# A decoder layer in split fp32: the residual held over the norm's factor, the last down blocks by seven products, one group summed in PSUM through ScalarE, and order constants by stage

## The chip, the cores and the metric

The kernel runs on one core of one Trainium2 chip. The metric is the device time of one execution in microseconds, with the median over several runs. TensorE (PE) multiplies, VectorE (DVE), ScalarE (ACT) and GpSimd (POOL) work on the tiles in between, and SyncE (SP) issues most of the DMA transfers. One execution was profiled; its span is shorter than its time by what lies before the first and behind the last instruction.

## The reference, cut to what matters

One step of a decoder layer for 512 prompt tokens and 8 x 4 sample tokens, 544 columns in all, with a model width of 1024 and a feed-forward width of 2816, in fp32:

```python
h = rmsnorm(x, norm_mix)
z = h @ w_in                                   # split into dilated attention and HGRN2
...
x = x + jnp.concatenate([att, o], axis=-1) @ w_out
c = rmsnorm(x, norm_cross)
...
x = x + co @ w_co                              # cross attention
u = rmsnorm(x, norm_ffn)
ug = u @ w_gate
up = jnp.concatenate([conv_buf.astype(ug.dtype), ug], axis=1)
conv = conv_b + sum(conv_w[j] * up[:, j:j + T] for j in range(CONV_W))
x = x + (jax.nn.silu(conv) * (u @ w_up)) @ w_down
...
yp = rmsnorm(yp, norm_final)
```

## The kernel before, in words

All activations lie transposed: a tile has 128 features as partitions and the 544 tokens as columns. x is held as eight tiles `xr` (m = 0 to 7), and the feed-forward's inner width of 2816 is 22 blocks of 128 (k = 0 to 21), whose activations are called `up`, and, once they are split for PE, `h0h`, `h0l` to `h21h`, `h21l`.

**Split products.** An fp32 product is made of three passes in PE's format fp32r: high by high, high by low and low by high (`passes`). So each operand is split: ACT casts the high part (a name that ends in h), DVE subtracts it for the low part (a name that ends in l). Some small products (norm sums, attention scores, the recurrence) are plain fp32 matmuls.

**Seven products.** Where two blocks of output rows and two halves of the columns (of `HT` = 272) meet, a two by two product of blocks is made by seven products in place of eight (the Winograd form of Strassen's method). `Pair` does this for gate and up, two output blocks at a time: the weight's sums S1 and S3 are made by DMA (a load by SP and an accumulating load on POOL's queue), S2 and S4 by DVE; the differences W, X, T, U, V of the right side are made once (`blocks`). The products are q1 to q7, with 12 matmuls each, in PSUM tiles called ps_a, ps_d, ps_c. For the first gate pair the weights are `wrg` (A11, A12; high `whg`, low `wlg`), `S1g`, `S2g`, `S3g` and their parts `S1g2h`, `S3g2h`, `S3g2l`; the products go to `ps_ag`.

**The feed-forward.** `ffn_in` gives the rows' factor r (tile `r_ux`, 1 over the root mean square, made by ACT as Exp of -0.5 times a Ln). Blocks 0 and 1 of gate and up are plain products, the others are pairs. `conv` takes a gate block (tile `ug`), applies the convolution's taps on ACT and DVE (tile `cv`), silu on ACT, and then multiplies by r once more (`weigh`), so that up's product needs no factor of its own; POOL fills the edges of `ug` and keeps its last columns (`last`). The down product is summed into x in groups of four k blocks (`DOWNS`; the last is k = 14 to 17), in two column cuts `CUTS` of 256 and 288, each with a DVE add of PSUM into `xr` (`down_half`), PSUM tile `ps_d`. These halves are laid between the products of the pairs by a fixed table.

**The end.** The last four blocks, k = 18 to 21 (`DOWN_LAST`), follow by `last_half(m, c)`: 12 matmuls for each m and column half, first all m of half 0 (288 columns), then half 1 (256), PSUM tile `ps_dz`. Each result is added to x on DVE, squared on ACT and summed over m (tile `acc_final`) by POOL, for the last m by DVE. `final(c)` adds the partitions up by two plain fp32 matmuls (`psr_final`), ACT makes the factor (`r_fin` and `r_final`: Ln, then Exp twice, once into PSUM), DVE and POOL make the outputs y, and SP and ACT issue the stores. `final(0)` comes after m = 2 of half 1. The very last half is added by PE onto a copy of x that ACT put into PSUM.

**What sets the order.** A recorder, `Tape`, takes every instruction as a step with its needs, and sets the order of each engine. PE's steps that are marked as main keep their written order; its other steps (mostly plain fp32) are put between them in bursts. `BURST` says how much such work must be ready for a burst and `PATIENCE` how long it may wait. `due` gives each step a time before which it has to begin: `MARGIN` is the room that it keeps ahead of a main step, and `LEAD` says how long ahead of its due time an engine may take a step, unless the step has a lead of its own (`lead=`, `tape.early`). All engines work off their queues in order, so a step that waits holds back all that stands behind it on its engine, DMA issues on SP and POOL included.

Almost all instructions go through one recording line (L638) and all DMA issues through another (L612), so the profile's groups are told apart by their tiles. In the changed kernel these are L650 and L624.

## Time and profile before

| what | value |
|---|---|
| median of 3 runs | 818.39 us (816.56 to 819.32) |
| profiled execution | 817.74 us |
| its span | 816.0 us, so 1.74 us lie outside |
| PE busy | 803.5 us, 98% |
| PE weight loads (PEld) | 755.0 us, 93% |
| DVE busy | 656.3 us, 80% |
| ACT busy | 424.7 us, 52% |
| POOL busy | 108.3 us, 13% |
| feed-forward with the last blocks | about 460 to 807.65 us |
| last blocks (ps_dz) | 782.57 to 807.65 us |

The page gives busy time and share of the span. Rows of a timeline give start, length, engine, line, operation, out<-in with shapes and count, and in brackets how long the engine idled before it and what ended that. Matmuls overlap: a row's own length, 0.28 us, is more than the step from one matmul to the next, which is what counts for time and is read from starts. In rows of windows a stretch is followed by busy us and count of PE, PEld, DVE, ACT and POOL, then PE's granted clock, the DMA engines' share and GB/s.

### The profile page before, as it was taken

The numbers are of one execution on the slowest core, as the hardware profiler recorded it, in microseconds if no ns is written. First come the engines' busy times: TensorE is split into PE (matmuls) and PEld (weight loads), VectorE is DVE, ScalarE is ACT, GpSimd is POOL, SyncE is SP. The second block draws the span as 40 slices with busy tenths as digits, with TensorE's granted clock in tenths as the row PEclk, the third lists the DMA queues.
The fourth block names the chain that finished last, engine by engine and source line by source line (L and its number), as shares of the span: only waits on it lengthen the run. The fifth ranks groups of instructions, "written<-read, shape, count | busy, mean of one in ns | idle before, by whom it ended". The sixth has DMA issues, their size and how long they took to land.

```text
span 816.0 us, 18919 instructions
## 1 busy us (share of the span) xinstructions
PE 803.5 (98%) x7515; PEld 755.0 (93%) x7515; DVE 656.3 (80%) x1486; ACT 424.7 (52%) x845; POOL 108.3 (13%) x186
## 2 busy tenths in 40 slices
PE   9999999999999999999999999999999999999996
PEld 9999986797889889999889999999999999999996
DVE  6986789987997987564679999997888788887854
ACT  7643346366558455454457656544454455445543
POOL 0020000010010000002300221222113111211013
PEclk9999999999999999999999999999999999999999
DMA  9439996956844444261732665555455565564403
GB/s 315 165 101 306 335 382 204 318 168 215 259 137 134 146 132 157 59 219 36 236 109 61 167 171 133 155 130 167 118 154 132 132 166 142 130 166 119 136 17 111
DMA packets 93065, 135.48 MB, mean 166 GB/s; under 512 B 6320, under 2 KB 60336, under 8 KB 92976
## 3 DMA queue, kind: packets, MB, share of 16 engines
q1 hardware_dynamic: 86208, 122.79, 46.9%
q0 software_dynamic: 5760, 10.49, 8.3%
q8 instruction: 59, 0.97, 0.5%
q10 hardware_dynamic: 1008, 0.99, 0.4%
q14 instruction: 30, 0.25, 0.1%
...
## 4 chain that ended last, share of the span: by engine, by line
PE 61%; DVE 4%; ACT 1%; DMA 1%; issue 0%; DVEq 0%
PE ps_d L638 13%; PE ps_ag L638 7%; PE ps_au L638 7%; PE ps_wo L638 6%; PE ps_cu L638 4%; PE ps_cg L638 4%; PE ps_co L638 3%; PE ps_dz L638 3%; PE ps_cq L638 3%; PE ps_dg L638 2%; PE ps_du L638 2%; PE ps_g L638 1%; DVE wl L638 1%; PE ps_cpo L638 1%; PE ps_cp L638 1%; PE ps_cv L638 1%
## 5 line engine op out<-in xcount | busy, mean ns | idle before, releaser
L638 ACT CAST wh<-wr 128x1024 fp32r<-128x1024 f32 (+1 forms) x54 | 46.4, 873 | 51.5 <-PE ps_z_i L638 10.8
L638 DVE TENSOR_TENSOR wl<-wr,wh 128x1024 fp32r<-128x1024 f32 (+1 forms) x54 | 55.2, 1030 | 3.0 <-ACT wh L638 2.8
L638 DVE TENSOR_TENSOR xr<-xr,ps_d 128x256 f32<-128x256 f32 x80 | 34.7, 434 | 13.7 <-PE ps_d L638 12.9
L638 POOL COPY last<-ug 128x2 f32<-128x2 f32 (+1 forms) x44 | 19.9, 479 | 129.2 <-DVE ug L638 129.2
L638 DVE SCALAR_TENSOR_TENSOR cv<-ug,vec,cv 128x560 f32<-128x560 f32 x44 | 35.2, 799 | 0.8
L638 ACT ACTIVATE cv<-ug,vec 128x560 f32<-128x560 f32 x22 | 18.8, 856 | 29.9 <-DVE ug L638 29.9
L638 POOL TENSOR_TENSOR hvm<-hsm,cs 64x512 f32<-64x512 f32 x4 | 5.5, 1386 | 160.4 <-ACT hsm L638 116.1
L638 DVE TENSOR_TENSOR cv<-cv,r_ux 128x512 f32<-128x512 f32 (+1 forms) x44 | 18.4, 436 | 3.4 <-ACT cv L638 3.0
L612 POOL DMA_DIRECT2D S1u<-in_w_up x10 | 8.6, 862 | 92.8 <-PE ps_au L638 62.0
L638 POOL TENSOR_SCALAR cp<-cp,cden 128x256 f32<-128x256 f32 x8 | 8.0, 999 | 93.2 <-DVE cden L638 93.0
L638 POOL COPY ug<-conv_state 128x16 f32<-128x16 f32 x22 | 18.4, 837 | 13.9 <-PE ps_co L638 5.8
L638 ACT ACTIVATE cv<-cv 128x560 f32<-128x560 f32 x22 | 14.8, 673 | 8.5 <-DVE cv L638 8.2
L638 DVE TENSOR_TENSOR keptg<-ps_cg,keptg 128x272 f32<-128x272 f32 x20 | 8.8, 440 | 12.7 <-PE ps_cg L638 12.2
L638 PE MATMUL ps_co<-coh,wh 128*128 128x256 f32 (+1 forms) x64 | 18.9, 295 | 0.0
L638 ACT ACTIVATE P<-P,mx 128x128 f32<-128x128 f32 (+3 forms) x32 | 17.6, 552 | 1.8 <-DVE mx L638 1.8
L638 PE MATMUL ps_co<-col,wh 128*128 128x256 f32 (+1 forms) x64 | 18.4, 288 | 0.0
L638 PE MATMUL ps_co<-coh,wl 128*128 128x256 f32 (+1 forms) x64 | 18.4, 288 | 0.0
L638 DVE TENSOR_TENSOR xr<-xr,ps_wo 128x256 f32<-128x256 f32 (+1 forms) x16 | 6.8, 436 | 13.7 <-PE ps_wo L638 13.6
L638 DVE TENSOR_TENSOR keptu<-ps_cu,keptu 128x272 f32<-128x272 f32 x20 | 8.8, 438 | 9.9 <-PE ps_cu L638 9.7
L638 DVE TENSOR_TENSOR xr<-xr,ps_dz 128x288 f32<-128x288 f32 (+1 forms) x15 | 6.6, 438 | 12.4 <-PE ps_dz L638 12.4
L638 PE MATMUL psdo<-st,dpt 128*32 128x256 f32 x224 | 16.3, 387 | 0.0
L638 ACT COPY keptg<-ps_ag 128x272 f32<-128x272 f32 x20 | 7.7, 386 | 16.3 <-PE ps_ag L638 16.2
...
## 6 DMA issues: line engine op xcount, KB each, us to landing
...
wd<-in_w_down SPq DMA_DIRECT2D x32, 256.0 KB, 3.4
...
```

What stands on the lines that cost most here:

```text
L612: return tape.put(engine, lambda: call(*args, **kw), outs, ins, 0.1, 0.3, size)
L638: return tape.put(engine, lambda: call(*args, **kw), outs, ins, length, lag, size, port, words)
```

## The change

1. **The residual over the factor.** `weigh` goes. The inner activations are thereby larger by 1/r for each token, and x is brought to the same scale: each `xr` tile is once multiplied by the root mean square (`rms_ffn`, made by ACT as one more Exp of the same Ln), after the pairs' differences have read it and ahead of its first down add. The final norm doesn't see a factor of a token, except in its epsilon, which is folded into the sum of squares: POOL rescales the sum of the ffn norm (`acc_ux`) by epsilon, adds a constant, and the last norm's sum is built on that tile.
2. **Last blocks.** The pairs m = (0,1), (2,3), (4,5) are made by seven products of 6 matmuls of 272 columns each; m = 6 and 7 stay plain. Their weight sums (tiles `wzS`) are made by 20 SP loads (with the plain ones) in place of 8 and 21 accumulating DMAs of 128 KB on POOL's queue; the right side's differences are `lX`, `lU`, `lT`, `lV`. `LAST_ORDER` gives the order of the products; `final(0)` stands ahead of the last two. All y of half 0 are made by DVE.
3. **Group 14.** For k = 14 to 17 ACT copies x into PSUM, PE adds to it, and ACT copies the sum back to `xr`; DVE adds nothing. All down halves are cut into 272 and 272 columns.
4. **Constants by stage.** `BURST`, `PATIENCE`, `LEAD` and `MARGIN` are taken from a table of ten stages of the planned time.

Instructions per engine: PE 6431 to 6413, DVE 1488 to 1467, ACT 802 to 843, POOL 191 to 211, SP 350 to 362.

```diff
-LAST_CUTS = ((0, 288), (288, 256))
+LAST_CUTS = ((0, HT), (HT, HT))
+LAST_ORDER = ((0, 1), (0, 2), (1, 1), (1, 2), (0, 6), (0, 7), (1, 6), (2, 1), (0, 4), (1, 7), (2, 2), (2, 6), (1, 4), (2, 7),
+              (0, 5), (1, 5), (2, 4), (0, 3), (2, 5), None, (1, 3), (2, 3))
...
-    BURST, PATIENCE, SLACK, LEAD, MARGIN = 0.77, 3.65, 12.0, 16.11, 3.44
+    SLACK = 12.0
+    STAGES = ((0.0, 1.05, 3.03, 18.1, 2.34), (60.0, 0.96, 2.87, 17.03, 5.98), (120.0, 1.23, 4.33, 13.64, 2.85),
...
+              (740.0, 0.66, 3.38, 13.88, 4.81))
...
     class SumSq:
...
-    ssq3 = SumSq("final", nc.gpsimd)
+    ssq3 = SumSq("final", nc.gpsimd, acc=ffn_in.ssq.acc)
+    nc.gpsimd.tensor_scalar(ssq3.acc[:, :N], ssq3.acc[:, :N], EPS, D / 128 * EPS * EPS, op0=ALU.mult, op1=ALU.add)
...
-        def weigh():
-            c = hid[j]
-            nc.vector.tensor_tensor(c[:, :SEQ], c[:, :SEQ], r_ffn[:, :SEQ], op=ALU.mult)
-            nc.vector.tensor_tensor(seg(c)[:, :, 0:4], seg(c)[:, :, 0:4], by_batch(r_ffn[:, SEQ:N]), op=ALU.mult)
...
     def down_half(k0, k1, m, c, split, deps):
-        n0, n = CUTS[c]
...
+        n0, n = HT * c, HT
+        on = k0 >= 14
...
+        def fill():
+            box["ps"] = PF(f"ps_d{k0}_{m}_{n0}")
...
+            nc.scalar.copy(box["ps"][:, :n], x[m][:, n0:n0 + n])
...
+        if m not in scaled:
+            scaled[m] = job(lambda: nc.vector.tensor_tensor(x[m][:, :N], x[m][:, :N], rms_ffn[:, :N], op=ALU.mult),
+                            *(d for told in read for d in told.values()), lead=40.0)
+        if k0 >= 14:
+            job(lambda: nc.scalar.copy(x[m][:, n0:n0 + n], box["ps"][:, :n]), p)
+        else:
+            job(lambda: add_to(m)(box["ps"], n0, n), p, scaled[m])
...
-    ON_POOL = (1, 3, 6), (1, 5)
+    k0, k1 = DOWN_LAST
+    ON_POOL = (), (1, 3)
...
+    def last_weights(p):
...
+        nc.gpsimd.dma_start(raw["S13"][:, 0:2, :], w[1][:, 0:2, :], accum_op=ALU.add)
+        nc.gpsimd.dma_start(raw["S13"][:, 2:4, :], w[1][:, 0:2, :], accum_op=ALU.add)
...
+        for to in (slice(0, 2), slice(2, 4)):
+            nc.sync.dma_start(raw["S24"][:, to, :], w[1][:, 0:2, :])
+        for to in (slice(0, 2), slice(2, 4)):
+            nc.gpsimd.dma_start(raw["S24"][:, to, :], w[1][:, 2:4, :], accum_op=ALU.add)
+            nc.gpsimd.dma_start(raw["S24"][:, to, :], w[0][:, 0:2, :], accum_op=ALU.add)
+        nc.gpsimd.dma_start(raw["S24"][:, 2:4, :], w[0][:, 2:4, :], accum_op=ALU.add)
...
+    PRODUCTS = {1: ("a", "A11", "B11"), 2: ("d", "A12", "B21"), 6: ("a", "S2", "U"), 7: ("c", "S3", "X"),
+                5: ("a", "S1", "T"), 4: ("c", "A22", "V"), 3: ("a", "S4", "B22")}
...
+        def product(self, i):
+            bank, wa, xb = PRODUCTS[i]
...
+            for m, c, op, ends in {1: ((m0, 0, ALU.add, False),), 2: ((m0, 0, ALU.add, True),),
+                                   6: ((m1, 0, ALU.subtract, False),),
+                                   7: ((m1, 1, ALU.add, False),), 4: ((m1, 0, ALU.add, True),),
+                                   5: ((m1, 1, ALU.subtract, True),), 3: ((m0, 1, ALU.add, True),)}[i]:
...
+                nc.vector.tensor_tensor(x[m][:, cut], x[m][:, cut], ps[:, :HT], op=op)
```

Where it moves instructions, at these places. First ACT at the start of the feed-forward, where the first gate pair's weights are cast (`whg` for q1, `S3g2h` for a later product); before:

```order
L638 ACTIVATE cv_1217<-ug_1214,vec 128x560
L638 CAST S1g2h<-S1g_1239 128x512
L638 CAST S3g2h<-S3g_1254 128x512
L638 CAST whg_1231<-wrg_1230 128x1024
L638 ACTIVATE cv_1217<-cv_1217 128x560
L638 CAST S2g2h<-S2g_1240 128x512
```

and now:

```order
L650 ACTIVATE cv_1217<-ug_1214,vec 128x560
L650 CAST S1g2h<-S1g_1239 128x512
L650 CAST whg_1231<-wrg_1230 128x1024
L650 ACTIVATE cv_1217<-cv_1217 128x560
L650 CAST S2g2h<-S2g_1240 128x512
L650 CAST S3g2h<-S3g_1254 128x512
```

The cast of S3g now stands behind those of the pair's other weights. DVE at the same place, now:

```order
L650 TENSOR_TENSOR S2g_1240<-S1g_1239,wrg_1230 128x512
L650 TENSOR_TENSOR up_1220<-ps_u_256_1222,cv_1211 128x256
L650 TENSOR_TENSOR up_1220<-ps_u_256_1222,cv_1211 128x32
L650 TENSOR_TENSOR S1g2l<-S1g_1239,S1g2h 128x512
L650 TENSOR_TENSOR wlg_1232<-wrg_1230,whg_1231 128x1024
L650 TENSOR_TENSOR S2g2l<-S2g_1240,S2g2h 128x512
L650 TENSOR_TENSOR up_1228<-ps_u_0_1229,cv_1217 128x256
L650 TENSOR_TENSOR S3g2l<-S3g_1254,S3g2h 128x512
```

Before, the last add to up_1220, S2g, S3g2l and wlg followed each other. Next, DVE from the last adds to x up to the second half's norm (the first y of half 1); before:

```order
L638 TENSOR_TENSOR xr_915<-xr_915,ps_dz_1_2046 128x256
L638 SCALAR_TENSOR_TENSOR y_0_2050<-xr_913,vec,r_final_2049 128x288
L638 SCALAR_TENSOR_TENSOR y_0_2051<-xr_915,vec,r_final_2049 128x288
L638 TENSOR_TENSOR xr_916<-xr_916,ps_dz_1_2055 128x256
L638 SCALAR_TENSOR_TENSOR y_0_2052<-xr_917,vec,r_final_2049 128x288
L638 SCALAR_TENSOR_TENSOR y_0_2053<-xr_918,vec,r_final_2049 128x288
L638 TENSOR_TENSOR xr_917<-xr_917,ps_dz_1_2057 128x256
L638 SCALAR_TENSOR_TENSOR y_0_2054<-xr_920,vec,r_final_2049 128x288
L638 TENSOR_TENSOR xr_918<-xr_918,ps_dz_1_2059 128x256
L638 TENSOR_TENSOR xr_919<-xr_919,ps_dz_1_2062 128x256
L638 TENSOR_TENSOR acc_final<-acc_final,sq_final_5_2060 128x256
L638 TENSOR_TENSOR acc_final<-acc_final,sq_final_6_2063 128x256
```

and now:

```order
L650 TENSOR_TENSOR xr_915<-xr_915,ps_az_2050 128x272
L650 SCALAR_TENSOR_TENSOR y_0_2081<-xr_913,vec,r_final_2080 128x272
L650 TENSOR_TENSOR xr_917<-xr_917,ps_az_2066 128x272
L650 SCALAR_TENSOR_TENSOR y_0_2082<-xr_914,vec,r_final_2080 128x272
L650 TENSOR_TENSOR acc_ux<-acc_ux,sq_final_5_2089 128x272
L650 SCALAR_TENSOR_TENSOR y_0_2083<-xr_915,vec,r_final_2080 128x272
L650 TENSOR_TENSOR xr_919<-xr_919,ps_z_1_2091 128x272
L650 TENSOR_TENSOR acc_ux<-acc_ux,sq_final_6_2090 128x272
L650 SCALAR_TENSOR_TENSOR y_0_2084<-xr_916,vec,r_final_2080 128x272
L650 SCALAR_TENSOR_TENSOR y_0_2085<-xr_917,vec,r_final_2080 128x272
L650 TENSOR_TENSOR acc_ux<-acc_ux,sq_final_7_2092 128x272
```

Five products y, three adds and three sums now alternate ahead of the second norm's sum; three more y follow. The last place is ACT's queue ahead of the last blocks (`ps_d_7` are the PSUM tiles of group 14's last m), now:

```order
L650 COPY ps_d_7_0_1997<-xr_920 128x272
L650 COPY xr_919<-ps_d_6_272_1988 128x272
L650 CAST wzS24h_2031<-wzS_2025 128x512
L650 CAST lXh<-lX 128x544
L650 COPY ps_d_7_272_1998<-xr_920 128x272
L650 CAST lUh<-lU 128x544
L650 CAST wzAh_2058<-wzA_2054 128x512
L650 CAST h21h<-up_1977 128x544
```

The cast of the summed weights S24 of the first pair stands there ahead of the fill of the last PSUM tile and of h21h.

More of the change, by code (lines that the diff above doesn't have):

```diff
@@ L384, in as_written, with at @@
         return self.mark("kept")
+    def at(self, t):
+        return [c for c in self.STAGES if c[0] <= t][-1][1:]
     def due(self):
@@ L550, in order @@
                     at = clock[0] + min(now - clock[1], 4.0)
-                    can = [s for s in waiting[e] if s.ready <= now + 1e-9 and s.begin <= at + (s.lead or self.LEAD) and fits(s)]
+                    ahead = self.at(clock[0])[2]
+                    can = [s for s in waiting[e] if s.ready <= now + 1e-9 and s.begin <= at + (s.lead or ahead) and fits(s)]
                     if can:
@@ L561, in order @@
                     first = now
-                if side and (burst or not main or sum(s.length for s in side) >= self.BURST
-                             or now - first > self.PATIENCE
+                enough, patience = self.at(clock[0])[:2]
+                if side and (burst or not main or sum(s.length for s in side) >= enough
+                             or now - first > patience
                              or min(s.begin for s in side) < clock[0] + now - clock[1]):
@@ L2303, in tile_decoder_step @@
     later.run()
-    r_fin, last_sq = A("r_fin"), A("sq_last")
-    hs, k = [hid[j] for j in range(*DOWN_LAST)], DOWN_LAST[1] - DOWN_LAST[0]
-    ys, last = {}, []
-    ON_POOL = (1, 3, 6), (1, 5)
+    r_fin, last_sq, ys = A("r_fin"), A("sq_last"), {}
+    k0, k1 = DOWN_LAST
+    ON_POOL = (), (1, 3)
     def y_at(m, c):
@@ new lines, in done, with plain_weights @@
+    def done(m, c):
+        cut = slice(HT * c, HT * c + HT)
+        if (m, c) == (5, 0):
+            nc.scalar.activation(last_sq[:, cut], x[m][:, cut], AF.Square)
+        else:
+            ssq3.add(x[m][:, cut], HT * c, nc.vector if (m, c) in ((3, 0), (2, 1), (4, 1), (6, 1)) else None)
+        if m in ON_POOL[c]:
+            nc.scalar.activation(y_at(m, c), x[m][:, cut], AF.Copy, scale=V("norm_final", m))
+    def plain_weights(m):
+        t, hi, lo = (A(f"{n}z{m}", [128, k1 - k0, 128], dt) for n, dt in (("wd", F32), ("wdh", F32R), ("wdl", F32R)))
+        nc.sync.dma_start(t, w_down[m][:, 128 * k0:128 * k1].rearrange("p (k c) -> p k c", c=128))
+        nc.scalar.copy(hi, t)
+        nc.vector.tensor_tensor(lo, t, hi.bitcast(F32), op=ALU.subtract)
+        return [(hi[:, i, :], lo[:, i, :]) for i in range(k1 - k0)]
@@ L2326, in last_half, with plain @@
+    def plain(m, c):
+        cut = slice(HT * c, HT * c + HT)
+        ps = PF(f"ps_z{m}_{c}")[:, :HT]
+        whole = (m, c) == (KT - 1, 1)
         if whole:
             tape.gate_at = len(tape.mains) - 1
-            nc.scalar.copy(ps[:, :n], x[m][:, cut])
+            nc.scalar.copy(ps, x[m][:, cut])
             tape.gate_at = None
+        tape.cut()
         with tape.main():
-            passes(ps, held[m], hs, n0, n, range(k), not whole, loose=whole)
+            passes(ps, held[m], [hid[j] for j in range(k0, k1)], HT * c, HT, range(k1 - k0), not whole, loose=whole)
+        tape.cut()
@@ L2344, in final @@
+        done(m, c)
     def final(c):
-        n0, n = LAST_CUTS[c]
-        cut = slice(n0, n0 + n)
+        cut = slice(HT * c, HT * c + HT)
         ps = PX(f"psr_final{c}")
         for i, sq in enumerate((ssq3.acc, last_sq)):
-            nc.tensor.matmul(ps[:, :n], C("ones"), sq[:, cut], start=i == 0, stop=i == 1)
-        nc.scalar.activation(r_fin[:, cut], ps[:, :n], AF.Ln, bias=eps, scale=1.0 / D)
-        r = PX(f"r_final{c}")[:, :n]
+            nc.tensor.matmul(ps[:, :HT], C("ones"), sq[:, cut], start=i == 0, stop=i == 1)
@@ L2353, in final @@
+        nc.scalar.activation(r_fin[:, cut], ps[:, :HT], AF.Ln, scale=1.0 / D)
+        r = PX(f"r_final{c}")[:, :HT]
         nc.scalar.activation(r, r_fin[:, cut], AF.Exp, scale=-0.5)
@@ L2362, in final @@
             (nc.scalar if c and m % 2 else nc.sync).dma_start(yT[128 * m:128 * m + 128, cut], out)
-    held = []
-    for m in range(KT):
-        t, hi, lo = (A(f"{n}z{m}", [128, k, 128], dt) for n, dt in (("wd", F32), ("wdh", F32R), ("wdl", F32R)))
-        with tape.early(12.0):
-            nc.sync.dma_start(t, w_down[m][:, 128 * DOWN_LAST[0]:128 * DOWN_LAST[1]]
-                              .rearrange("p (k c) -> p k c", c=128))
-            nc.scalar.copy(hi, t)
-            nc.vector.tensor_tensor(lo, t, hi.bitcast(F32), op=ALU.subtract)
-        held.append([(hi[:, i, :], lo[:, i, :]) for i in range(k)])
-        last_half(m, 0)
-    for m in range(KT):
-        last_half(m, 1)
-        if m == 2:
+    pairs_z = [LastPair(p) for p in range(3)]
+    last, held = [], {}
+    for m in (6, 7):
+        with tape.early(20.0):
+            held[m] = plain_weights(m)
+        plain(m, 0)
+    with tape.early(20.0):
+        sides_of = last_blocks()
+    for at in LAST_ORDER:
+        if at is None:
+            tape.cut()
             with tape.main():
                 final(0)
+            continue
+        p, i = at
+        if i == 1:
+            with tape.early(20.0):
+                pairs_z[p].w = last_weights(p)
+        if at == (0, 5):
+            tape.gate_at = len(tape.mains) - 1
+            nc.sync.dma_start(conv_out, last2)
+            nc.scalar.preload_act_table_set(LN_SET)
+            tape.gate_at = None
+        pairs_z[p].product(i)
+    plain(6, 1)
+    plain(7, 1)
+    tape.cut()
     with tape.main():
```

127 lines of the change are left out of this document (89 added, 38 removed).

## The prediction

> **What bounds the kernel now.** I read the page first, for the share of each engine and the clock.
>
> ```profile
> span 816.0 us, 18919 instructions
> PE 803.5 (98%) x7515; PEld 755.0 (93%) x7515; DVE 656.3 (80%) x1486; ACT 424.7 (52%) x845; POOL 108.3 (13%) x186
> PEclk9999999999999999999999999999999999999999
> ```
>
> PE is busy for all but 12.5 us of the span and its granted clock never falls, so the questions are how many matmuls are left, and where PE stands. The windows by stage say where.
>
> ```profile
> 280.00:300.00 20.00, 19.39 (x253) 15.85 (x254) 19.84 (x51) 7.76 (x15) 1.93 (x2) 1.00 0.37 97
> ...
> 480.00:760.00 280.00, 280.00 (x2237) 280.00 (x2236) 237.37 (x480) 138.94 (x247) 56.43 (x106) 1.00 0.56 143
> ```
>
> The columns are PE, PEld, DVE, ACT and POOL busy time, then clock and DMA. From 480 to 760 us (the feed-forward) PE stands for nothing: whatever DVE is spared there buys nothing, and only a matmul fewer shortens it. At 280 us, in the mixing stages, PE does stand (0.61 of 20 us), and DVE is busy there for 19.84. The waits of PE, summed by what ended them:
>
> ```profile
> PE psL L638 <- DVE mx L638: 0.8, 1, 0.8
> PE ps_z_q L638 <- DVE z_q L638: 0.7, 1, 0.7
> PE psU L638 <- ACT hkt L638: 0.6, 1, 0.6
> PE ps_ag L638 <- DVE wlg L638: 0.6, 1, 0.6
> PE psu L638 <- issue: 0.4, 1, 0.4
> PE pst_hk L638 <- DVE hk L638: 0.3, 1, 0.3
> PE psin L638 <- DVE hin L638: 0.3, 1, 0.3
> ```
>
> Apart from the first matmuls of all, this is 3.7 us: 0.6 at the start of the feed-forward (ps_ag), 3.1 in the mixing stages. The end is read in the chain of waits (start, length, what):
>
> ```profile
> 757.02 1.51 PE ps_au L638 x12
> ...
> 782.57 17.05 PE ps_dz L638 x132
> 799.62 0.97 PE psr_final L638 x4
> 800.59 7.06 PE ps_dz L638 x60
> ...
> 807.67 1.17 PE psr_final L638 x4
> ```
>
> The last blocks are 192 matmuls in 24.1 us without a gap, and after 807.67 everything is a fixed tail of norm, scale and store.
>
> **Part 1: fewer matmuls in the last blocks.** Three pairs by seven products of 6 matmuls are 126, and the plain m = 6, 7 are 48: 174 in place of 192, all of 272 columns. The chain gives 1.51/12 = 0.126 us for 272 columns (ps_au) and (17.05 + 7.06)/192 = 0.1256 for the mix of 288 and 256, the same. So 18 x 0.1256 = **-2.26 us** at PE's end.
>
> Part of it is given back on DVE. The rows of the tail:
>
> ```profile
> 801.61 0.94 DVE L638 SCALAR_TENSOR_TENSOR y<-xr,vec,r_final 128x288 f32<-128x288 f32 x2 [1.53 <-ACT r_final L638]
> ...
> 806.62 0.99 DVE L638 TENSOR_TENSOR acc_final<-acc_final,sq_final 128x256 f32<-128x256 f32 x2
> 807.69 0.39 ACT L638 ACTIVATE sq_last<-ps_dz 128x256 f32<-128x256 f32 x1 [0.53 <-PE ps_dz L638]
> ```
>
> Before, the first half's norm came with 60 matmuls (7.06 us) to go, and DVE's last sum ended at 807.61, before PE did. In the change 36 matmuls are to go (36 x 0.1256 = 4.5 us), no y of half 0 is on POOL, and DVE's order has, between that norm and the last sum that the second norm waits for, five y (0.47 each), three adds to x (0.43, the mean of group 14's row below, two of them on PE's results) and three sums (0.49). From the first norm's factor, which I put 2.0 us after its matmuls start as before (799.62 to 801.61), at 799.85 + 2.0 = 801.85, these are 5 x 0.47 + 3 x 0.43 + 3 x 0.49 = 5.1 us: 807.0 if all of it lies behind that factor, 806.4 with the first add, whose result of PE comes at 801.8, ahead of it and some overlap at the ends. The three other y's fall into the second norm. The second norm's second operand, the square of the last block, is ready at 805.4 + 0.02 + 0.39 = 805.8, so **+0.6 us** with bounds 0 and +1.2. Sixteen more columns in each late y are below 0.1 us together: +0.1.
>
> The products need their operands in time. Their adds (15 become 22) have four and more products between them; the differences of blocks lX, lU, lT, lV and the low parts of six more weights are 8 + 4 + 6 = 18 DVE operations. The cover is DVE's idle time from 782 on, and 60 us of the feed-forward before:
>
> ```profile
> 760.00:782.00 22.00, 22.00 (x178) 22.00 (x177) 19.18 (x41) 10.72 (x19) 0.98 (x4) 1.00 0.36 108
> 782.00:800.00 18.00, 18.00 (x140) 17.89 (x139) 5.95 (x14) 7.37 (x15) 4.75 (x6) 1.00 0.00 1
> ```
>
> DVE idles 12 of 18 us there, so I cost them at nothing; without that cover 18 x 0.6 = 11 us would show. In 760 to 782 us DVE has 2.8 us left, which is the place to watch.
>
> **Part 2: the residual held over the row factor, and group 14 on ACT.** DVE loses the 44 products with r_ux and the adds of group 14, gets eight products x by 1/r; ACT gets 32 copies.
>
> ```profile
> L638 DVE TENSOR_TENSOR cv<-cv,r_ux 128x512 f32<-128x512 f32 (+1 forms) x44 | 18.4, 436 | 3.4 <-ACT cv L638 3.0
> L638 DVE TENSOR_TENSOR xr<-xr,ps_d 128x256 f32<-128x256 f32 x80 | 34.7, 434 | 13.7 <-PE ps_d L638 12.9
> L638 ACT COPY keptg<-ps_ag 128x272 f32<-128x272 f32 x20 | 7.7, 386 | 16.3 <-PE ps_ag L638 16.2
> ```
>
> That is -18.4 and -16 x 0.434 = -6.9 on DVE, +8 x 0.7 = +5.6 (0.7 from the 128x512 product with two tiles, 0.69 below), and 32 x 0.386 = +12.4 on ACT, which is half idle. PE stands for neither in 480 to 760 us, so **0**, and no cover is lost: DVE keeps 43 of 280 us and more. The one POOL operation on the sum of squares is hidden too: nobody waits for it before the first square of the last blocks, some 300 us later.
>
> At the start of the feed-forward it does count. ACT, DVE and PE there:
>
> ```profile
> 456.97 0.52 DVE L638 TENSOR_TENSOR up<-ps_u,cv 128x256 f32<-128x256 f32 x2 [0.18 <-PE ps_u L638]
> 457.71 0.62 ACT L638 CAST S3g2h<-S3g 128x512 fp32r<-128x512 f32 x1 [2.17 <-DMA S3g<-in_w_gate]
> 458.23 1.05 ACT L638 CAST whg<-wrg 128x1024 fp32r<-128x1024 f32 x1
> 459.31 1.23 DVE L638 TENSOR_TENSOR wlg<-wrg,whg 128x1024 fp32r<-128x1024 f32 x1 [0.26 <-ACT whg L638]
> 460.46 0.69 DVE L638 TENSOR_TENSOR cv<-cv,r_ux 128x512 f32<-128x512 f32 x1
> 459.73 0.29 PE L638 MATMUL ps_ag<-ux0l,whg 128*128 128x272 f32 x1
> 460.60 0.39 PE L638 MATMUL ps_ag<-ux0h,wlg 128*128 128x272 f32 x1 [0.58 <-DVE wlg L638]
> ```
>
> PE waits for wlg, it for whg, and whg stood behind S3g2h, which waited 2.17 us for a DMA that POOL had issued. In the change whg stands ahead of S3g2h; it is then free at about 457.05, when the PE products that held its tile are read (456.97), and wlg can follow at 458.1. On DVE S2g, two adds and S1g2l stand ahead of it (0.69 + 0.52 + 0.69 = 1.9 from 456.7), so it ends at 459.8, while PE needs it one step after 459.73, at 459.86. The stall of 460.60 - 459.86 = 0.74 all but goes: **-0.65 us**, bounds 0 and -0.74. What is late next is S3g2l, needed two products later, 3 us.
>
> **Part 3: order constants.** From 300 us to the tail PE's order is the same as before. From 20 to 300 us it is rearranged, and the groups of plain fp32 matmuls among the split ones go from 45 to 42. What one such group costs in change of form is seen at the tail:
>
> ```profile
> 800.21 0.49 PE L638 MATMUL ps_dz<-h18h,wdhz 128*128 128x256 f32 x1
> 800.54 0.28 PE L638 MATMUL ps_dz<-h18l,wdhz 128*128 128x256 f32 x1
> 800.66 0.28 PE L638 MATMUL ps_dz<-h18h,wdlz 128*128 128x256 f32 x1
> ```
>
> The first step is 0.33, the next 0.12: 0.21 us lost, so 3 x 0.2 = **-0.6 us** (0 if the three merged groups had lain in waits). What the rearranging does to the 3.1 us of waits there the trace of before cannot show: between -3.1 (all gone) and +3.1 (as many again, with DVE at 19.8 of 20 us); I take **0**, since the work of each engine there is the same.
>
> **The sum**, against the profiled execution of 817.74 us (span 816.0 and 1.74 outside): -2.26 + 0.6 + 0.1 - 0.65 - 0.6 = -2.8, 814.9. The median of the runs, 818.39, lies 0.65 above that execution, so I forecast 815.6 us.
>
> **Rivals.** (a) The accumulating DMAs come late; slower. Sums of weight blocks are made by 21 DMAs of 128 KB on POOL's queue, between its last copies and its first sum of squares. How such transfers stand in the trace (KB each, us to landing) in 720 to 800 us, then single rows at the start of the feed-forward and POOL's idle time before that sum:
>
> ```profile
> S1g<-in_w_gate POOLq DMA_DIRECT2D x1, 256.0 KB, 4.8
> S3g<-in_w_gate POOLq DMA_DIRECT2D x1, 256.0 KB, 6.3
> ```
>
> ```profile
> 447.98 1.04 POOL L612 DMA_DIRECT2D S1g<-in_w_gate  x1 [0.36 <-PE ps_g L638]
> 454.91 0.62 ACT L638 CAST S1g2h<-S1g 128x512 fp32r<-128x512 f32 x1 [0.28 <-DMA S1g<-in_w_gate]
> ...
> 786.83 0.81 POOL L638 TENSOR_TENSOR acc_final<-acc_final,sq_final 128x288 f32<-128x288 f32 x1 [25.30 <-ACT sq_final L638]
> ```
>
> POOL is free from 786.83 - 25.30 = 761.5. Eleven issues of about 1.0 us, and one landing of 3 to 5 that the last of them waits behind, put the last sum of pair 0 at 761.5 + 11 + 3 to 5 = 775.5 to 777.5 us. ACT casts it (wzS24h) behind the copy of the m = 6 result, which PE ends 36 matmuls before the last blocks, 782.57 - 36 x 0.126 = 778.0; behind that cast stand the cast of lX, the fill of the last PSUM tile of the group, for 781.1, and h21h, which PE needs by 782.5. So it may start as late as 781.1 - 0.39 - 2 x 0.62 = 779.5, 2 to 4 us of slack. Had each of four serial landings the 6.9 us of the second fence (447.98 to 454.9) in place of 4.8, it would come 4 x 2.1 = 8.4 us later; less 3 us of slack PE stands for 5.4: 821.0. It decides once a landing takes over 4.8 + 3/4 = 5.5 us. For it: the 6.3 above. Against: the transfers are half as large and the DMA engines a third busy (0.36).
>
> The Trainium skill ("SBUF — State Buffer", SBUF: two separate sides) says that descriptors of a DMA issued from GpSimd cannot be written while VectorE holds the port that they share, and gives 620 ns that became 3100 ns. By its rule rival (a) is the likelier, the more so as DVE is busy 19.18 of 22 us just there; the issue of 1.04 us at 447.98 shows no fivefold stretch, so I leave (a) a small chance.
>
> (b) The rearranged stage saves its waits as well: 815.6 - 3.1 = 812.5. For it: half of these waits end at DVE, and a later lead suits them; against: DVE's work there is not less.
>
> (c) The rearranged stage costs what the rest gains, the places where DVE limits PE being only moved: new waits of 2.8 us in 120 to 300 us, where DVE's 19.84 of 20 leaves it no room: 818.4, no change. For it: every wait of PE there ends at DVE or ACT, so any instruction of theirs put later shows in full.
>
> **How the numbers follow.** Chances: forecast 0.46, (a) 0.12, (b) 0.20, (c) 0.22. What a measurement of this kernel can tell from no change is 0.3%, 2.46 us, so faster begins below 815.9, just above the forecast. Faster: 0.6 of the forecast's share (its bounds are uneven, +1.9 if stall, groups and y's all go the wrong way) and all of (b): 0.48. Slower: (a) and 0.02 of (c): 0.14. Same: 0.38. The range goes from 811.8 (below (b) by the bounds of the stall and the sums, 0.7) to 820.0, which leaves out the worse part of (a); the forecast's own is 814.0 to 817.5.
>
> **What would show it.** Right: 174 matmuls from about 782.5 to 805.4 less what was gained earlier, with no row of PE waiting; wlg no longer in PE's waits; the second psr_final waiting for a sum on DVE, about 0.6 us. Rival (a) would show as ACT idle before a cast of the summed weights with a DMA as the releaser, and PE waiting at ps_d or the first z; (b) and (c) as the sum of PE's waits between 20 and 300 us. The forecast is wrong if the span to the start of the feed-forward (ps_ag, 459.6) moves by over 1.5 us, or if PE stands between 480 and 782 us.

## The result

| | median | runs |
|---|---|---|
| before | 817.55 us (816.56 to 819.32) | 22 |
| changed | 819.81 us (818.40 to 821.53) | 22 |

The ratio is 1.0028, with an interval of 1.0021 to 1.0035: the change is a little slower, by 2.3 us, where 815.6 us and faster had been forecast. The profiled execution of the changed kernel took 818.40 us, the fastest of its 22; its median lies 1.4 us above it.

The page of the changed kernel, its span and the busy time of the engines:

```profile
span 816.5 us, 18993 instructions
PE 803.7 (98%) x7497; PEld 754.5 (92%) x7497; DVE 654.4 (80%) x1465; ACT 438.3 (54%) x886; POOL 126.5 (15%) x206
```

PE has 18 matmuls fewer and is as busy as before; no share on this page tells why. The waits of PE, summed by what ended them, do (us in total, times, longest):

```profile
PE ps_d L650 <- ACT ps_d L650: 2.1, 2, 1.2
PE ps_first L650 <- DVE zero L650: 1.1, 1, 1.1
PE ps_du L650 <- ACT ps_du L650: 0.7, 1, 0.7
PE psr_final L650 <- DVE acc_ux L650: 0.6, 1, 0.6
PE ps_z_q L650 <- DVE z_q L650: 0.5, 1, 0.5
PE pst_hk L650 <- DVE hk L650: 0.4, 1, 0.4
PE psL L650 <- ACT hAT L650: 0.2, 1, 0.2
```

The wait for wlg is gone, those of the mixing stages are down from 3.1 to 1.1 us, and the 0.6 us ahead of the last norm is there as forecast. New are 2.8 us in two tiles that PE waits for ACT to fill, `ps_du` and `ps_d`, all between 660 and 782 us, where PE had stood for nothing. What ACT was doing there, by its timeline (the bracket: idle time before it and what ended that):

```profile
658.27 0.62 ACT L650 CAST S3u14h<-S3u 128x512 fp32r<-128x512 f32 x1 [2.76 <-DMA S3u<-in_w_up]
...
659.84 1.05 ACT L650 CAST whg<-wrg 128x1024 fp32r<-128x1024 f32 x1
660.79 0.38 ACT L650 COPY ps_du<-ps_au 128x272 f32<-128x272 f32 x1
...
724.43 0.62 ACT L650 CAST S3u18h<-S3u 128x512 fp32r<-128x512 f32 x1 [1.79 <-DMA S3u<-in_w_up]
...
726.94 0.38 ACT L650 COPY ps_d<-xr 128x272 f32<-128x272 f32 x1
...
780.26 0.62 ACT L650 CAST wzS13h<-wzS 128x512 fp32r<-128x512 f32 x1 [2.18 <-DMA wzS<-in_w_down]
780.78 0.38 ACT L650 COPY ps_d<-xr 128x272 f32<-128x272 f32 x1
```

Three times ACT stands idle with a cast at the head of its queue that waits for an accumulating DMA, and a copy that PE needs stands behind it: the first product sum of a pair (`ps_du`), the first fill of group 14 and the last but one (`ps_d`). Over the span ACT is busy for only 54%. DMA transfers in 644 to 662 us, before (first row) and after (second), and in 760 to 782 us after (KB each, us from issue to landing); then the queues' share of the 16 engines' time, and the window's row whose like before had a DMA share of 0.36. The share after, 1.10, is the sum of the queues' shares:

```profile
S3u<-in_w_up POOLq DMA_DIRECT2D x1, 256.0 KB, 4.9
```

```profile
S3u<-in_w_up POOLq DMA_DIRECT2D x1, 256.0 KB, 7.3
...
wzS<-in_w_down POOLq DMA_DIRECT2D x19, 128.0 KB, 5.7
...
q0 software_dynamic: 2129, 1.95, 57.3%
q1 hardware_dynamic: 3155, 3.84, 52.0%
...
760.00:782.00 22.00, 21.10 (x169) 20.88 (x168) 14.86 (x32) 13.52 (x30) 17.47 (x25) 1.00 1.10 264
```

Where the time went is seen by the start of the same PE instruction in both traces:

| place | before | after | after - before | step |
|---|---|---|---|---|
| behind the mixing stages (ps_cv) | 310.06 | 309.29 | -0.76 | -0.76 |
| first gate pair (ps_ag, third matmul) | 460.60 | 459.00 | -1.60 | -0.84 |
| product behind the fill of ps_du | 662.06 | 661.22 | -0.84 | +0.76 |
| first fill of group 14 | 726.72 | 727.38 | +0.66 | +1.50 |
| last fill of group 14 (second matmul) | 780.95 | 783.12 | +2.16 | +1.50 |
| last norm's second matmul | 808.21 | 808.84 | +0.63 | -1.53 |

Gains about as large as the forecast's terms are all in the table (-0.6 for the constants, -0.65 at the gate pair, -2.26 + 0.6 in the last blocks), and three stalls of 3.8 us in all have been put on top. The list of waits counts 2.8 us of these: it counts from the end of the row before, some 0.16 us after the next matmul would have started, and the first step behind a wait is 0.23 us in place of 0.12.

### The profile page after: what moved, and what is told of

Read it like the earlier page. It is cut to its first block, busy times and chain, and to the rows that moved or that the text cites. A ratio compares the mean times of both kernels' runs of the same rounds, so it can differ in the third digit from the quotient of the medians.

```text
span 816.5 us, 18993 instructions
## 1 busy us (share of the span) xinstructions
PE 803.7 (98%) x7497; PEld 754.5 (92%) x7497; DVE 654.4 (80%) x1465; ACT 438.3 (54%) x886; POOL 126.5 (15%) x206
## 4 chain that ended last, share of the span: by engine, by line
PE 84%; DVE 6%; DMA 5%; ACT 3%; issue 1%; POOL 0%; SPq 0%; DVEq 0%; POOLq 0%; ACTq 0%
PE ps_d L650 11%; PE ps_au L650 7%; PE ps_ag L650 7%; PE ps_wo L650 6%; PE ps_cg L650 3%; PE ps_co L650 3%; PE ps_cq L650 3%; PE ps_cu L650 3%; DMA S3u<-in_w_up 3%; PE ps_z_i L650 2%; PE ps_z_v L650 2%; PE ps_du L650 2%; PE ps_dg L650 2%; PE psd L650 2%; PE psdo L650 2%; PE ps_z_Q L650 2%
## 5 line engine op out<-in xcount | busy, mean ns | idle before, releaser
L650 DVE TENSOR_TENSOR wl<-wr,wh 128x1024 fp32r<-128x1024 f32 (+1 forms) x54 | 53.4, 1002 | 2.4 <-ACT wh L650 2.2
L650 DVE TENSOR_TENSOR xr<-xr,ps_d 128x272 f32<-128x272 f32 x64 | 27.6, 432 | 13.1 <-PE ps_d L650 12.7
L650 POOL COPY last<-ug 128x2 f32<-128x2 f32 (+1 forms) x44 | 23.6, 565 | 91.6 <-DVE ug L650 91.4
L624 POOL DMA_DIRECT2D wzS<-in_w_down x21 | 18.6, 1748 | 11.7 <-PE ps_au L650 7.7
L650 ACT COPY keptu<-ps_au 128x272 f32<-128x272 f32 x20 | 7.7, 384 | 14.8 <-PE ps_au L650 14.4
L650 POOL COPY ug<-conv_state 128x16 f32<-128x16 f32 x22 | 14.1, 640 | 10.1 <-DMA conv_state<-in_conv_in 2.8
```

The lines of the kernel that those rows point to most:

```text
L624: return tape.put(engine, lambda: call(*args, **kw), outs, ins, 0.1, 0.3, size)
L650: return tape.put(engine, lambda: call(*args, **kw), outs, ins, length, lag, size, port, words)
```

## The experiments

The experiments' times are medians; each is compared with runs of the kernel before on the same chip (817.3 to 817.7 us, so a few tenths between two experiments say nothing).

**Each part undone, or alone.** First the constants.

```diff
-    STAGES = ((0.0, 1.05, 3.03, 18.1, 2.34), (60.0, 0.96, 2.87, 17.03, 5.98), (120.0, 1.23, 4.33, 13.64, 2.85),
...
+    STAGES = ((0.0, 0.77, 3.65, 16.11, 3.44),)
```

> The four order constants of before in all stages, the rest of the change kept. Theory (the constants only bring the gain before 460 us): 0.76 us of the mixing stages and 0.8 us of the stall at the first gate pair come back, S3u still late: 820.5 to 821.5. Rival (the constants for 500 to 740 us put the pairs' loads late): the waits at 660 and 727 us go, 818.5 to 819.5.

824.33 us, ratio 1.0092 (1.0068 to 1.0115). Neither theory had it: without the table the stalls grow, ps_d to 4.2 us and ps_du to 1.6. So the table doesn't put the pairs' loads late; it takes off 4.5 us, less than half of it ahead of 460 us. The other way round, the table in the kernel before:

```diff
-    BURST, PATIENCE, SLACK, LEAD, MARGIN = 0.77, 3.65, 12.0, 16.11, 3.44
+    SLACK = 12.0
+    STAGES = ((0.0, 1.05, 3.03, 18.1, 2.34), (60.0, 0.96, 2.87, 17.03, 5.98), (120.0, 1.23, 4.33, 13.64, 2.85),
...
```

> The kernel before with the table of constants by stage and nothing else of the change. Theory (the constants gain 0.8 us in the mixing stages and 0.8 at the first gate pair; the late S3u comes from the other parts): 816.0 to 816.5 against 817.6 before, PE waits for neither ps_du nor ps_d. Rival (the constants themselves put the S3u transfers late): 817.5 to 818.5 with waits near 660 and 727 us.

815.65 us, ratio 0.9979 (0.9968 to 0.9990), and PE waits neither at ps_du nor at ps_d. At the first gate pair it stands at 458.99, 1.6 us earlier than before, as in the changed kernel. So the constants alone are worth 2.0 us by the medians and 1.6 by the two profiled executions, against 1.25 in my terms for them together. The median lies below the expected 816.0 to 816.5.

The residual over the factor alone (the cuts of 272 columns stay, which change no matmul count):

```diff
-    STAGES = ((0.0, 1.05, 3.03, 18.1, 2.34), (60.0, 0.96, 2.87, 17.03, 5.98), (120.0, 1.23, 4.33, 13.64, 2.85),
...
+    STAGES = ((0.0, 0.77, 3.65, 16.11, 3.44),)
...
-        on = k0 >= 14
+        on = False
...
-    for m in (6, 7):
-        with tape.early(20.0):
+    for m in range(KT):
+        with tape.early(12.0):
             held[m] = plain_weights(m)
         plain(m, 0)
```

> The change with all eight m plain in the last blocks, group 14 added by DVE and one set of constants, so the residual over the factor alone (and the 272-column cuts, a re-timed end). Theory (with DVE's products by r gone, the queues are packed anew and the pairs' S3u lands late against PE): 1.5 to 2.5 us above before, 819.0 to 820.0, PE waiting at ps_du. Rival (harm comes only with group 14's copies or the weight sums): 817.3 to 818.0, as before.

819.63 us, ratio 1.0026 (1.0017 to 1.0036). Its profiled execution is the fastest of its ten (818.85), and PE waits 0.5 us there at ps_du, near 729 us, behind a cast of S3u18 for which ACT stood idle for 2.6 us. Taking 9.6 us of work off DVE (656.3 to 646.7) goes with 2.0 us more. POOL's issue of the sum that the profile of the change showed late, S3u14:

```profile
652.94 0.86 POOL L621 DMA_DIRECT2D S3u<-in_w_up  x1 [4.42 <-DMA S3u<-in_w_up]
```

Before, it stood at 650.47. PE is at the same place at the first gate pair in both (460.61 and 460.60), so with the residual over the factor this transfer is issued 2.5 us later against PE. The same kernel with the loads of the pairs' S1 and S3 allowed 3 us earlier:

```diff
-        load, box = load_a(name, a, 4, lead=11.0)
+        load, box = load_a(name, a, 4, lead=14.0)
...
-        return job(lambda: None, job(accumulate, load, lead=12.0)), box
+        return job(lambda: None, job(accumulate, load, lead=15.0)), box
```

> residual_alone with the pairs' loads of S1 and S3 up to 3 us earlier. Theory (its harm is the late S3u): 819.6 - 2.0 = 817.6, as before, no wait of PE at ps_du. Rival (the re-timed end or the longer queue costs): 818.5 or more.

817.40 us, ratio 0.9996 (0.9987 to 1.0006): all of it is gone, with the wait at ps_du; that issue is now at 647.38. So the residual's harm was the lateness of these loads, as far as the interval of 0.8 us to either side can tell. (The kernel before with the earlier leads was not run; PE waits nowhere between 480 and 782 us there.) The same edit in the whole change:

> The loads and accumulating DMAs for the gate and up pairs' S1 and S3 may be issued 3 us earlier (leads 11 and 12 become 14 and 15). Theory (S3u of the pairs at 658 and 724 us lands too late because its transfer is issued late against PE): the PE waits at ps_du (0.7 us) and ps_d near 727 us (1.2 us) go, -1.5 to -2 us; the cast of S3g returns ahead of whg at the start of the feed-forward, which may bring back up to 0.7 us: 818.0 to 819.0. Rival (the transfer itself is stretched by the other loads, however early): 819.8 or more.

817.75 us, ratio 1.0001 (0.9991 to 1.0010). The waits near 660 and 727 us are gone, and the time is 2.1 us down, 0.25 below the expected 818.0 to 819.0. The 0.7 us at the first gate pair are back, since there the early sum pulled S3g's cast ahead of whg again; in the kernels below the first gate pair keeps its leads. What is left is the last one, longer than the 0.9 us that it had in the change's profile:

```profile
PE ps_d L650 <- ACT ps_d L650: 2.3, 1, 2.3
PE ps_first L650 <- DVE zero L650: 1.1, 1, 1.1
PE ps_ag L650 <- DVE wlg L650: 0.7, 1, 0.7
```

**The last blocks.** All eight m plain again, the rest kept:

> All eight m of the last four blocks by plain products, 192 matmuls of 272 columns, no weight sums, the rest of the change kept. Theory: +2.26 us of matmuls, -0.6 us of DVE's sums ahead of the last norm, and the stall ahead of the last blocks goes (-1.5 to -2.5): 819.0 to 820.0, no wait of PE near 781 us. Rival (the stall there comes from group 14's copies on ACT): 821.0 to 821.5 with the stall still there.

818.52 us, ratio 1.0015 (1.0004 to 1.0025). It has 18 matmuls more than the change and is 1.3 us faster, 0.5 below the expected range; no wait near 781 us. With both edits:

> All eight m plain in the last blocks, and S1 and S3 of all pairs but the first gate pair up to 3 us earlier; the rest of the change kept. Theory (no sums by DMA at the end, S3u early): 818.5 less about 2 for the waits near 660 and 727 us: 816.3 to 817.0, no wait at ps_d. Rival (group 14's fills on ACT are late by themselves): the wait near 727 us stays, 817.5 to 818.5.

815.74 us, ratio 0.9982 (0.9973 to 0.9991), 0.6 below the expected 816.3 to 817.0, and PE waits nowhere behind 300 us. And group 14 back on DVE in that kernel:

```diff
-        on = k0 >= 14
+        on = False
```

> As early_and_plain, with group 14 added by DVE again: no fills and no copies by ACT. Theory (ACT and DVE both have room once S3u is in time): 815.7, no difference. Rival (fills and copies cost PE even then, or DVE's 16 adds do): 0.5 to 1 us either way.

815.85 us, ratio 0.9985 (0.9975 to 0.9996): 0.1 us apart, nothing. The fills on ACT cost nothing once nothing ahead of them waits. In the changed kernel two of the three stalls stand at such fills; the change with its late transfers and group 14 on DVE was not run.

Is it the sums of weight blocks that make the seven products lose? The one experiment that leaves part of the computation out:

```diff
-        nc.sync.dma_start(raw["S13"][:, 0:2, :], w[1][:, 2:4, :])
...
+        nc.sync.dma_start(raw["S13"], w[1])
         nc.sync.dma_start(raw["A22"], w[1][:, 2:4, :])
...
-        nc.gpsimd.dma_start(raw["S24"][:, 2:4, :], w[0][:, 2:4, :], accum_op=ALU.add)
+        nc.sync.dma_start(raw["S24"], w[1])
```

> The whole change with the pairs' loads early (the first gate pair's left as they are), and in the last three pairs the sums of weight blocks left out: S13 and S24 are plain loads by SP (256 KB each), so the outputs of m = 0 to 5 are not the reference's, while every cast, subtraction, product and add stays. Theory (the accumulating DMAs are what makes the seven products lose): no wait near 780 us, 18 matmuls fewer than early_and_plain at 815.7, 0.6 given back at the last norm: 814.1. Rival (DVE can't prepare and take up the products in time whatever the sums cost, as in early_and_pool_sums): waits at ps_cz or ps_dz for DVE, 815.7 to 816.5.

814.11 us, ratio 0.9963 (0.9949 to 0.9977), as expected; that it fits to the tenth is luck with such intervals. It is 1.63 us below early_and_plain, against -2.26 + 0.6 + 0.1 = -1.56. The traces agree: from the first gate pair's third matmul to the last norm's second PE takes 347.23 us in early_and_plain and 345.63 here, 1.60 less. The stage's row has PE without a gap, at a DMA share of 0.43 in place of 1.10:

```profile
760.00:782.00 22.00, 22.00 (x178) 22.00 (x177) 16.10 (x34) 16.75 (x37) 0.00 (x0) 1.00 0.43 135
782.00:800.00 18.00, 18.00 (x143) 17.85 (x142) 15.07 (x36) 10.47 (x24) 8.31 (x10) 1.00 0.01 1
```

All of ACT's and DVE's work of the seven products is in these rows, so it fits; what does not fit is the transfers that make the sums. Fewer pairs by seven products, the sums still by DMA:

```diff
-LAST_ORDER = ((0, 1), (0, 2), (1, 1), (1, 2), (0, 6), (0, 7), (1, 6), (2, 1), (0, 4), (1, 7), (2, 2), (2, 6), (1, 4), (2, 7),
-              (0, 5), (1, 5), (2, 4), (0, 3), (2, 5), None, (1, 3), (2, 3))
+LAST_ORDER = (('m', 6, 0), ('m', 7, 0), ('p', 0, 1), ('p', 0, 2), ('m', 4, 0), ('p', 0, 6), ('p', 1, 1), ('p', 1, 2), ('p', 0, 7), ('m', 5, 0), ('p', 1, 6), ('p', 0, 4), ('p', 1, 7), ('p', 1, 4), ('p', 0, 5), ('p', 1, 5), ('p', 0, 3), None, ('p', 1, 3), ('m', 4, 1), ('m', 5, 1), ('m', 6, 1), ('m', 7, 1))
```

(here 'm' is a plain half and 'p' a product of a pair; the kernel with one pair has products of pair 0 alone, and m = 2 to 7 plain.)

> As early_and_plain, with m = 0 to 3 of the last blocks by seven products (14 accumulating DMAs); final(0) with 54 matmuls to go. Theory: 12 matmuls fewer, 815.7 - 1.5 = 814.2 if 14 accumulations still land in time; by the share of the DMA engines (1.08 with 21 of them) I rather expect a wait of about 1 us: 815.2. Rival (the lateness comes from the first pair's chain alone, whatever follows): as one_pair's stall, 815.5 to 816.5.

817.58 us, ratio 1.0007 (0.9998 to 1.0016), PE waiting 2.1 us at ps_d.

> As early_and_plain, but m = 0 and 1 of the last blocks by seven products (7 accumulating DMAs in place of 21); final(0) with 60 matmuls to go. Theory: 6 matmuls fewer, nothing late: 815.7 - 0.75 = 815.0. Rival (even one pair's sums by DMA come late): a wait of 0.5 to 2 us near 780 us, 815.5 to 817.

818.36 us, ratio 1.0013 (0.9999 to 1.0027), PE waiting 0.5 us at each of ps_d, ps_az and ps_cz. Both lie above either range, though the waits that the rivals named are there: a third of the transfers is late as well. POOL's issues for the one pair, and ACT's cast of their result:

```profile
757.28 0.86 POOL L623 DMA_DIRECT2D wzS<-in_w_down  x1 [1.17 <-DMA wzS<-in_w_down]
...
760.91 0.86 POOL L623 DMA_DIRECT2D wzS<-in_w_down  x1 [1.73 <-DMA wzS<-in_w_down]
763.07 0.86 POOL L623 DMA_DIRECT2D wzS<-in_w_down  x1 [1.29 <-DMA wzS<-in_w_down]
765.53 2.64 POOL L623 DMA_DIRECT2D wzS<-in_w_down  x3 [1.60 <-DMA wzS<-in_w_down]
768.40 0.86 POOL L623 DMA_DIRECT2D wzS<-in_w_down  x1 [0.22 <-issue]
```

```profile
774.07 0.62 ACT L649 CAST wzS24h<-wzS 128x512 fp32r<-128x512 f32 x1 [1.44 <-DMA wzS<-in_w_down]
```

The first of the seven is issued at 757.28 and the last lands at 774: 17 us, in which POOL waits for a landing at four of the five places. By the code three of them follow one another in one half of S24, behind a load. So the chain is long even with a third of the transfers. (one_pair has two further waits in the last blocks themselves, where its products follow each other in one PSUM tile; so its time isn't that of the chain alone.)

**The sums made otherwise.** By DVE from two plain loads per pair, and by POOL:

```diff
-        raw = {n: A(f"wz{n}{p}", [128, 4, 128]) for n in ("A", "S13", "S24")}
+        raw = {n: A(f"wz{n}{p}", [128, 4, 128]) for n in ("A", "B", "S13", "S24")}
...
-        nc.gpsimd.dma_start(raw["S13"][:, 0:2, :], w[1][:, 0:2, :], accum_op=ALU.add)
+        nc.sync.dma_start(raw["B"], w[1])
...
+            nc.vector.tensor_tensor(to, u, v, op=ALU.add)
```

> The weight sums of the last pairs are made by 12 DVE adds of 128x256 from two plain loads per pair; the 21 accumulating DMAs and 6 SP loads go, nothing else of the program's order in PE changes. Theory (sums by DMA land late, ACT's queue stands behind them): the stall of 1.5 us ahead of the last blocks goes, -1.5 to -2.5 us against the changed kernel's 819.8, so 817.3 to 818.3, and PE waits at ps_d only near 727 us. Rival (ACT simply has too many instructions there: fills of group 14 and casts): 819.8 stays and ps_d still waits near 781 us.

819.64 us, ratio 1.0023 (1.0010 to 1.0037), a miss of the 817.3 to 818.3: no DMA is waited for near 781 us, but PE waits 1.2 us at ps_cz for DVE, and 2.0 at ps_d near 727. With POOL and the loads early:

> The pairs' loads early as in early_and_plain, and the last pairs' weight sums by 12 POOL adds of 128x256 (about 0.8 us each) from two plain loads per pair in place of 21 accumulating DMAs; everything else of the change. Theory: both stalls go, 819.8 - 2.0 - 1.5 = 816.3, down to 815.3 with what the landings' scatter costs; the last norm's 0.6 us stays. Rival (POOL's adds stand against DVE for the port and are late, or ACT is full): a wait of 1 us or more near 781 to 790 us stays, 817.5.

817.47 us, ratio 0.9998 (0.9988 to 1.0008), the rival's time. No wait at ps_d, but 1.2 us at ps_cz and 0.6 at ps_dz, for DVE's adds to x. DVE makes the low parts of the summed weights from 782.41 to 795.33 us there, in the last blocks themselves; with the sums left out it began with them at 776.69. Why they come so late, though POOL's last add starts at 776.56, is not shown. Next the sums went into the tile of S1 and S3, which two accumulations make side by side, and S2 and S4 follow by two adds once S1 and S3 are cast. All these loads may also be issued 6 us earlier:

```diff
+        raw["S24"], raw["A22"] = raw["S13"], A(f"wzA22{p}", [128, 2, 128])
...
-        for to in (slice(0, 2), slice(2, 4)):
-            nc.sync.dma_start(raw["S24"][:, to, :], w[1][:, 0:2, :])
...
+            if n == "S24":
+                nc.gpsimd.tensor_tensor(t[:, 0:2, :], t[:, 0:2, :], raw["A"][:, 0:2, :], op=ALU.add)
+                nc.gpsimd.tensor_tensor(t[:, 2:4, :], t[:, 0:2, :], raw["A"][:, 2:4, :], op=ALU.add)
...
-            with tape.early(20.0):
+            with tape.early(26.0):
```

> The whole change with the pairs' loads early; of the last pairs' sums only S1 and S3 are made by accumulating DMAs (two side by side per pair, 6 in place of 21), and S2 and S4 by two POOL adds of 128x256 in the tile of S1 and S3 after these are cast. Theory (the chain of serial landings is what is late): no DMA as releaser of ACT near 775 us, 814.1 as with the sums left out, up to 815 with POOL's adds. Rival (any preparation is too much for DVE and ACT between 760 and 800 us): waits at ps_cz or ps_dz for DVE as in early_and_pool_sums, 816.5 to 817.5.

815.67 us, ratio 0.9980 (0.9969 to 0.9991).

> As early_s24_by_pool with the two adds per pair on DVE (0.36 us each, 2.2 us in all). Theory: as there, 814.1 to 815; DVE has 20 of 22 us to do before the last blocks, so if DVE bounds the last blocks this one is slower than the one with POOL by 1 us or more.

815.98 us, ratio 0.9986 (0.9976 to 0.9997). In neither does ACT wait for an accumulating DMA any more. That does not single out the chain of serial landings: the edit also takes away 15 of the 21 accumulations and lets the rest start earlier. All 21 with the earlier start alone were not run; for the chain speaks one_pair, whose seven transfers were late. But both kernels are where early_and_plain is, not at 814.1: in the last blocks PE now waits for DVE, a few tenths at a time (ps_dz 0.3, ps_cz 0.2, ps_az 0.2 with POOL's adds), and DVE, busy for 15.07 of 18 us with the sums left out, is as busy there as PE:

```profile
782.00:800.00 18.00, 17.20 (x130) 16.32 (x129) 17.20 (x37) 8.79 (x18) 7.74 (x9) 1.00 0.00 1
```

(This profiled execution took 818.00 us, 2.3 more than its median. The excess lies ahead of the stages compared: from the first gate pair's third matmul to the last norm's second PE takes 347.55 us, 0.3 more than in early_and_plain.) Each theory holds for half: no cast waits for a sum, and what the saved matmuls bring is given back, at least in part in waits for DVE. Between the two engines for the adds the difference is 0.3 us, within the intervals.

Last the 0.6 us ahead of the second half's norm:

```diff
-    ON_POOL = (), (1, 3)
+    ON_POOL = (1, 3, 6), (1, 3)
```

> early_s24_by_pool with the first half's y for m = 1, 3 and 6 on POOL as before the change. Theory (five y and three sums queue on DVE ahead of the second half's norm): PE's wait of 0.5 us at psr_final goes to 0.1 or less, 815.7 - 0.5 = 815.2. Rival (the stores of y, not the norm, set the end): 815.7.

815.58 us, ratio 0.9974 (0.9963 to 0.9984): PE's wait at psr_final falls from 0.5 to 0.2 us, the median by 0.1, which the intervals do not tell from nothing; the theory's 815.2 is not reached.

**The scatter.** The changed kernel, profiled a second time:

> The changed kernel, profiled once more. Theory (its 3 us between fastest and slowest run are landings of accumulating DMAs that PE ends up waiting for): the waits at ps_du and ps_d differ from the 0.7 and 2.1 us of the first profile by as much as the span differs from 816.5, and the waits outside 640 to 790 us are the same within 0.3 us.

Its span is 817.9 us, 1.4 above the first profile's, and its time 819.77 is close to the median. PE's waits for ps_d, and the waits of ACT for DMAs between 640 and 790 us:

```profile
PE ps_d L650 <- ACT ps_d L650: 3.7, 2, 2.2
PE ps_first L650 <- DVE zero L650: 1.1, 1, 1.1
PE ps_ag1v L650 <- ACT rg1v L650: 0.9, 1, 0.9
PE psr_final L650 <- DVE acc_ux L650: 0.6, 1, 0.6
```

```profile
ACT wzS13h L650 <- DMA wzS<-in_w_down: 2.9, 1, 2.9
ACT S3u18h L650 <- DMA S3u<-in_w_up: 2.8, 1, 2.8
ACT S3u14h L650 <- DMA S3u<-in_w_up: 2.1, 1, 2.1
```

At the first gate pair it is at 459.10, 0.1 behind the first profile; at the last norm 1.37 behind. So the difference arose between them, and of the same waits the later two are longer: where the first profile had 1.79 us of ACT idle ahead of S3u18h and 2.18 ahead of wzS13h, these are 2.8 and 2.9; ahead of S3u14h it is 2.1 against 2.76, and PE no longer waits at ps_du. The expectation held in part. PE's waits at ps_du and ps_d together grew by 0.9 us, the span by 1.4. And the mixing stages have a wait of 0.9 us (ps_ag1v) that the first profile lacked, though PE is only 0.1 us later at 310 us. Nor do two profiles explain the spread of the runs: the kernel before, without such waits, spreads 2.8 us over 22 runs, the changed one 3.1.

## Why the prediction was wrong

The forecast was a change of -2.8 us, and +2.3 was measured. Two steps failed: the residual over the factor, put at nothing, and rival (a), put at a chance of 0.12. Of the two signs of being wrong that I had named, one came: PE stands between 480 and 782 us. Term by term:

- **The last blocks, -2.26 + 0.6 + 0.1:** right, and so are their parts, once the operands are in time. sums_left_out against early_and_plain gives -1.63, the trace of the change -1.53, the wait at the last norm 0.6.
- **The first gate pair, -0.65:** right, -0.84 in the trace with the constants' table, and pair_sums_early, which puts S3g's cast ahead again, has the wait of 0.7 back. The cause is the order on ACT and comes with the table, not with the residual: constants_alone is there at the same time.
- **The constants, -0.6 and 0 for the waits:** -0.76 in the mixing stages, close to the forecast by luck. The 0 for the waits was wrong: up to 310 us PE stood for 4.67 us before and stands for 2.43 now, 2.2 less. But up to the same matmul its rows are busy for 1.5 us more, in place of 0.6 less. The windows before and after:

```profile
0.00:310.00 310.00, 305.33 (x3544) 265.44 (x3544) 265.12 (x676) 170.38 (x345) 18.66 (x31) 1.00 0.68 218
```

```profile
0.00:310.00 310.00, 307.57 (x3548) 267.55 (x3549) 266.69 (x681) 171.75 (x349) 19.11 (x31) 1.00 0.68 220
```

  So rival (b) was right that waits go, and most of what they gave was lost again, as (c) had it, though not in new waits. What made the rows longer stays open.
- **Group 14 on ACT, 0:** right by itself (815.74 and 815.85), but not in the change, where 3.0 of the 3.8 us of stalls stand at its fills. For the same late S3u18 PE waits 0.5 us in residual_alone, without fills, and 1.2 in plain_last_blocks, with them.
- **The residual over the factor, 0 ("PE stands for neither in 480 to 760 us, so 0, and no cover is lost"):** this step failed, by 2.0 us (819.63 alone). I looked at the engines' busy time, and at what each engine has to spare. What was late was not work but a transfer, the pairs' S3u: a load by SP, then an accumulating DMA by POOL, then ACT's cast. Before, that cast did not wait, but it followed the landing closely (POOL's issue, then ACT's casts, by the timelines of before):

```profile
650.47 0.86 POOL L612 DMA_DIRECT2D S3u<-in_w_up  x1 [4.38 <-ACT wd_0h L638]
```

```profile
656.54 0.62 ACT L638 CAST wd_1h<-wd 128x512 fp32r<-128x512 f32 x1
657.06 0.62 ACT L638 CAST S3u14h<-S3u 128x512 fp32r<-128x512 f32 x1
```

  With 4.9 us to land it was in at 655.4, 1.7 us ahead of the cast. After, that room was used up from three sides: PE and with it ACT were 1.6 us further on, the accumulation was issued 0.5 us later (650.97), and it took 2.4 us longer, just behind three loads that SP had issued in the microsecond before; that these stretched it was not tried. 1.6 + 0.5 + 2.4 - 1.7 = 2.8, which is ACT's 2.76 us of idle time; 0.76 of them reach PE. That the load's place decides is shown (residual_early, pair_sums_early), and so is that it stands later against PE with the residual alone (652.94 in residual_alone). Why the order comes out so once the DVE work is gone is not.
- **Rival (a), chance 0.12:** it is the other part of the loss, 1.50 of the 3.8 us in the table, and should have had a far larger chance. I named the mechanism and the queue behind it rightly, and priced it wrongly at one point: "the DMA engines a third busy (0.36)" is a row of before, in which the change's own 21 accumulations and 12 added loads are not. After it is 1.10. A landing takes 5.7 us, above the 5.5 from which I had said that it decides. ACT waited for S13, not S24; with the pairs' loads early (pair_sums_early) it was S24 as I had said, with ACT idle for 3.6 us.
- **Range:** its upper end of 820.0 holds the measured time, but the chance of slower was 0.14. The forecast also started from a median of three runs, 818.39; that of 22 is 817.55.

The two rules of the Trainium skill that bear on these transfers came out differently. "DMA: Bandwidth & Descriptors" (Anatomy of one DMA — SWDGE (gpsimd) path) gives 2.0 us + bytes/436e3 for a transfer issued from GpSimd, which makes an estimate of 2.3 us for 128 KB; the accumulating ones here took 5.7 at the median, so the measurement decides. The port rule of "SBUF — State Buffer" (SBUF: two separate sides), by which I had said that rival (a) would be the likelier, told the right outcome; whether by its mechanism is doubtful. The Trainium skill tells it there of VectorE operations in a 2-port mode, with a copy as the example, and DVE's 27 rows in 760 to 782 us are TENSOR_TENSOR (25) and SCALAR_TENSOR_TENSOR (2). The issues themselves stayed at about 0.86 us. The engines' share of 1.10 and the serial landings are there as causes too, and no run here separates them.

Faster than both kernels, with the whole result computed, are constants_alone (815.65, ratio 0.9979), early_and_plain (0.9982), early_plain_dve14 (0.9985), early_s24_by_pool (0.9980), early_s24_by_dve (0.9986) and early_pool_y (815.58, ratio 0.9974, interval 0.9963 to 0.9984). Their medians lie within 0.4 us of each other: the table of constants carries the gain, and with the pairs' loads early the rest of the change no longer costs.
